# Stored low parts on the sync engine's DMA queue, their high parts from ScalarE

## The chip, the cores and the metric

The kernel runs on one core of a Trainium2 chip. The metric is the time of one execution in device microseconds; the median of several runs is compared. TensorE (PE) does the matmuls, VectorE (DVE) and ScalarE (ACT) the element-wise work, GpSimd (POOL) issues the DMAs that convert or accumulate, and SyncE (SP) issues the others.

## The reference

Two layers, each a mixer and an FFN, on x of 256 positions by 1024 features, in float32:

```python
for i in range(DEPTH):
    h = rms_norm(x, norm_mix[i])
    proj = einsum(h, w_in[i])      # qa ka va qb kb vb c_val c_gate qm, 256 columns each
    o_a = moba_attention(rope(norm(qa)), rope(norm(ka)), va)      # 4 heads of 64
    o_b = dilated_attention(rope(norm(qb)), rope(norm(kb)), vb)
    u = c_val * sigmoid(c_gate)
    o_c = silu(layer_norm(causal_depthwise_conv(u, conv_w[i]))) @ w_conv_out[i]   # 31 taps
    o_m = softmax(norm(qm) @ km.T) @ vm      # km, vm: from mem, with w_mem_kv[i]
    x = x + group_rms_norm([o_a, o_b, o_c, o_m]) @ w_out[i]
    h = rms_norm(x, norm_ffn[i])
    gate, val = split(causal_depthwise_conv(h @ w_up[i], ffn_conv_w[i]))   # 3 taps
    x = x + (silu(gate) * val) @ w_down[i]
```

## The kernel before, in words

**Three matmuls for one.** Every projection is made from a high and a low part of each operand, high·high + high·low + low·high (`mm3`). Weights come in units of 128 x 2048 float32, in two halves of 128 x 1024 (512 KB): `up0` to `up21` and `dn0` to `dn10` for the FFN, `qka`, `cg`, `qkb`, `cv`, `vv`, `qm` and `wo0` to `wo3` for a mixer (a pair such as `qka` is two units), and the small `co`. Three rings of SBUF slots hold halves: `st` (6 slots) as loaded, `wh` (7) the high parts, `wl` (7) the low parts.

**Three ways for a weight** (`get`, L725). The usual one: SP loads `st`, ACT copies it to `wh` in fp32r, DVE writes `wl` = `st` − `wh`; I call this last instruction the split of the half. The units in SOFT (L34): POOL loads `wh` with a converting DMA, ACT writes `wl` = −`wh`, and POOL's second DMA accumulates the weight onto it. The units in SPILL (L38) are for layer 1 alone: `wo1`, `wo0`, `qka` and `wo2`, ten halves. In FFN steps 3 to 12 of layer 0, one half a step, `spill` (L685) loads it, splits it, and stores the low part in a DRAM tile `sl` (`store`, L488, on POOL's queue). In layer 1 POOL loads the high part from the weights (`wh<-in_w`, converting) and the low part from the DRAM tile (`wl<-sl`).

**The stages.** The mixer of a layer (L1131) runs projections and attention in the order of ORDER (L44), the conv module's 31 taps on DVE beside them, and then the output projection `w_out` in three passes: groups b and a (PASSES' first entry, with `wo1` and `wo0`), memory (`wo3`), conv (`wo2`). The FFN (`ffn`, L1173) has 22 steps, each with an up projection, a gate, and the down projection of three steps earlier (LAG). Step 8 of layer 0 also makes the memory keys and values of layer 1 (`mem_kv`).

**What sets the order.** The whole program is first recorded as operations. A list scheduler (`schedule`, L492) then plans every engine's order from estimated durations, priorities (`key`) and free slots; it is rerun with priorities from the plan (`improve`, ITERS), and the best plan is emitted in that order. `get` and the spills put operations ahead by lowering `key`. SP's DMAs are chained in the order in which the program is recorded (`dma`, L475, through `dma_prev`), so SP's queue is never reordered; POOL's DMAs (`soft`, `store`) take any place that the plan gives them. A slot is free when its last use ends, in the plan 6.6 us later where that was a DMA of POOL (L568).

Instructions appear at L624 of `emit`, which issues all of them, but for the attention's matmuls (L622) and ACT's table loads (L618).

Of the kernel before, what the change touches and what calls it, by code (L numbers as in the profile page):

```python
# [10 lines left out]
F32 = mybir.dt.float32  # L11
F32R = mybir.dt.float32r
AF = mybir.ActivationFunctionType
ALU = mybir.AluOpType

P = 128
# [3 lines left out]
DEPTH = 2  # L20
# [9 lines left out]
HALF = UNIT // 2  # L30
# [5 lines left out]
RAW = ()  # L36

SPILL = ('wo1', 'wo0', 'qka', 'wo2')  # L38
SPILL_AT, SPILL_STEP = (3, 1)
LAG = 3  # L40

# [4 lines left out]
MEM_AT = 8  # L46
# [30 lines left out]
def unit_order():  # L77
    names = []
    for l in range(DEPTH):
        for s in ORDER[l]:  # L80
            names += [(l, s)] if s not in PAIRS or s == "mem" else []
            names += [(l, f"{s}{j}") for j in range(2)] if s in PAIRS else []
        for i, gs in enumerate(PASSES):
            if i == CO_AT:
                names += [(l, "co")]
            names += [(l, f"wo{g}") for g in gs]
        for i in range(NPAIR):
            names.append((l, f"up{i}"))
            if i == MEM_AT and l + 1 < DEPTH:
                names += [(l + 1, "mem"), (l + 1, "mem0"), (l + 1, "mem1")]  # L90
            if i >= LAG and (i - LAG) % 2 == 0:
                names.append((l, f"dn{(i - LAG) // 2}"))
        names += [(l, f"dn{j}") for j in range((NPAIR - LAG + 1) // 2, NPAIR // 2)]
    return names
# [224 lines left out]
LAT_CAST, LAT_ADD = 6600.0, 6600.0  # L319
# [4 lines left out]
class Rec:  # L324
# [160 lines left out]
        kw = dict(accum_op=ALU.add) if add else {}  # L485
        return self.op("pool", "dma_start", (out, src), kw, [out] if add else [], [out], 2200.0)

    def store(self, out, src):  # L488
        return self.op("pool", "dma_start", (out, src), {}, [src], [out], 2200.0)


    def schedule(self, slots):  # L492
        engs = ("pe", "act", "dve", "pool", "dma")
# [27 lines left out]
        while len(order) < len(self.ops):  # L521
            best = None
            for e in engs:
                cand = []
                for o in ready[e]:
                    t = possible(o)
                    if t is not None:
                        if o.table is not None and o.table != table[0]:
                            cand.append((t + TABLE_WAIT, o.key + TABLE_KEY, o.n, o, t))
                        else:  # L530
                            cand.append((t, o.key, o.n, o, t))
                if not cand:
                    continue
                t0 = min(c[0] for c in cand)
                c = min((c for c in cand if c[0] <= t0 + 1e-6), key=lambda c: (c[1], c[2]))
                if best is None or c[0] < best[0]:
                    best = c
            if best is None:
                raise RuntimeError("stuck: " + str([(e, [(o.meth, o.label, [(t.name, t.slot) for t in o.tiles])
                                                          for o in ready[e][:6]]) for e in engs]))  # L540
            o, t = best[3], best[4]
            ready[o.eng].remove(o)
            for l in o.tiles:
                if l.slot is None:
                    f = slot_free[l.tag]
                    f.sort(key=lambda x: x[:2])
                    l.slot, gate = f.pop(0)[1:]
                    o.gate.extend(gate)
                    turn[l.tag] = max(turn.get(l.tag, 0), l.seq + 1)
            dur = o.dur  # L550
            if o.table is not None and o.table != table[0]:
                dur += TABLE
                table[0] = o.table
            if o.eng == "pe":
                w = int(t // HAM)
                if w and busy.get(w - 1, 0.0) < COLD * HAM:
                    dur *= 2
                b = min(dur, (w + 1) * HAM - t)
                busy[w] = busy.get(w, 0.0) + b
                busy[w + 1] = busy.get(w + 1, 0.0) + dur - b  # L560
            o.start, o.end = t, t + dur
            free_at[o.eng] = o.end
            order.append(o)
            for l in o.tiles:
                l.left -= 1
                l.ops.append(o)
                if l.left == 0:
                    e = max(p.end + (LAT_CAST if p.eng == "pool" and p.meth == "dma_start" else 0.0) for p in l.ops)  # L568
                    slot_free[l.tag].append((e + LAT_X, l.slot, tuple(l.ops)))
            for q in o.nxt:  # L570
                q.wait -= 1
                q.ready = max(q.ready, o.end + q.prev[o])
                if q.wait == 0:
                    ready[q.eng].append(q)
# [76 lines left out]
class Kern:  # L651
# [33 lines left out]
    def spill(self, i):  # L685

        names = []
        for n in SPILL:
            names += [f"{n}{j}" for j in range(2)] if n in PAIRS else [n]
        if i >= 2 * len(names):  # L690
            return
        n, h = names[i // 2], i % 2
        r = self.r
        o = UOFF[(1, n)] * P
        src = self.d["w"][o:o + UNIT * P].rearrange("(p c) -> p c", p=P)[:, h * HALF:(h + 1) * HALF]
        st = self.t("st", [P, HALF], f"sp{n}{h}")
        r.dma(st, src, P * HALF * 4)
        hi, lo = self.t("wh", [P, HALF], f"sph{n}{h}", F32R), self.t("wl", [P, HALF], f"spl{n}{h}", F32R)
        self.split(hi, lo, st)
        d = self.t("sl", [P, HALF], f"sl{n}{h}")  # L700
        r.store(d, lo.bitcast(F32))
        self.spilled.setdefault(n, []).append((src, d))

    def unit(self, tag, cols, name, dtype=F32):
# [20 lines left out]
    def get(self, l, n, convert=True):  # L725
# [11 lines left out]
        soft = convert and spilled is None and (n in SOFT[l] or n[:-1] in SOFT[l]) and (l, n) not in self.staged  # L737
        if spilled is not None:
            hi, lo = self.unit("wh", cols, f"wh{l}{n}", F32R), self.unit("wl", cols, f"wl{l}{n}", F32R)
            self.r.key -= self.AHEAD  # L740
            for h, parts in enumerate(spilled):
                c = slice(h * HALF, (h + 1) * HALF)
                for out, src in zip((hi, lo), parts):
                    self.r.soft(out[:, c], src)
            self.r.key = save
            return hi, lo
        if not soft:
# [383 lines left out]
    def mixer(self, l, st, after):  # L1131
# [5 lines left out]
        for i, n in enumerate(ORDER[l]):  # L1137
# [24 lines left out]
            if 3 not in ys and "qm" in done and self.kv is not None:  # L1162
                base = r.key
                ys[3] = self.group_norm(self.attention(done["qm"], *self.kv, None, "m"), l, 3)
                self.kv = None
        for i, gs in enumerate(PASSES):
            if i == CO_AT:
                key, r.key = r.key, base
                ys[2] = self.group_norm(self.conv_out(l, y, self.get(l, "co")), l, 2)
                r.key = key  # L1170
            self.w_out(l, [(g, ys[g]) for g in gs], after if i == len(PASSES) - 1 else None)

    def ffn(self, l, st, after):  # L1173
# [14 lines left out]
        for i in range(NPAIR):  # L1188
# [2 lines left out]
                r.act(low[:, m, :], ps[:, 1, :], AF.Copy)  # L1191
                r.tt(us[:, m, :], ps[:, 0, :], low[:, m, :], ALU.add)
            if i == MEM_AT and l + 1 < DEPTH:
                self.kv = self.mem_kv(l + 1)
                self.gains(l + 1)
            if l == 0 and i >= SPILL_AT and (i - SPILL_AT) % SPILL_STEP == 0:
                self.spill((i - SPILL_AT) // SPILL_STEP)
            r.tt(us, us, st["rx"].twice(), ALU.mult)
            t = self.t2("tq")
            for c in range(2):  # L1200
# [19 lines left out]

    def build(self):
        r = self.r
        self.next_unit, self.staged, self.spilled = 0, {}, {}
        self.kv = None
        self.X = self.t("X", [P, NC, 256], "X")
        self.cst = self.t("cst", [P, NCST], "cst")
# [121 lines left out]
```

## Time and profile before

| | us |
|---|---|
| median of 3 runs (lowest to highest) | 623.24 (622.92 to 625.08) |
| the profiled execution | 623.19 |
| its span | 621.4 |
| PE busy | 608.0 (98% of the span) |
| DVE busy | 536.7 (86%) |
| ACT busy | 449.6 (72%) |
| POOL busy | 34.3 (6%) |

The span runs from the first to the last recorded instruction. PE was granted full clock throughout. Names such as `wh<-st` read "output from input", with the program's buffer names; in the orders below they carry the number of the buffer, so that one buffer can be followed.

### The profile page before, as it was taken

The page shows a single profiled execution, that of the slowest core. Times are in us where ns is not written, and L with a number is a line of the kernel's source. Part 1 is how long each engine was busy: PE and PEld are TensorE (multiplying, and loading weights), DVE is VectorE, ACT ScalarE, POOL GpSimd, SP SyncE. Part 2 cuts the span into 40 slices and gives each one's busy share as a digit, 9 for nine tenths or more (in the row PEclk, how much of TensorE's full clock was granted, in tenths as well). Part 3 has the DMA queues.
Part 4 walks back from the last instruction along what each step waited for, and adds up shares of the span by engine and source line. Part 5 has one row for each costly group of instructions (what it writes and reads, how often), then busy time and mean ns, then how long its engine had stood idle before and what let it go on. Part 6 is the DMA issues. An engine that isn't in the chain of part 4 may idle for free.

```text
span 621.4 us, 10750 instructions
## 1 busy us (share of the span) xinstructions
PE 608.0 (98%) x3884; PEld 537.0 (86%) x3884; DVE 536.7 (86%) x1048; ACT 449.6 (72%) x874; POOL 34.3 (6%) x63
## 2 busy tenths in 40 slices
PE   8999998999999999999999999899999999999997
PEld 5877876999998899999998878689899999999997
DVE  5899996899989999998869589849999888888874
ACT  6888969688776986766648488796776766666751
POOL 0001021000000000000020232100000000000000
PEclk9999999999999999999999999999999999999999
DMA  7987584676996899665685699606665565555401
GB/s 249 357 265 174 190 214 95 162 229 226 322 334 220 311 330 306 217 202 183 187 287 187 172 235 309 200 4 237 201 197 183 196 200 187 187 181 181 150 2 68
DMA packets 37493, 129.50 MB, mean 208 GB/s; under 512 B 4288, under 2 KB 5056, under 8 KB 37440
## 3 DMA queue, kind: packets, MB, share of 16 engines
q1 hardware_dynamic: 29664, 100.50, 48.7%
q0 software_dynamic: 7776, 28.32, 16.3%
q8 instruction: 30, 0.49, 0.3%
q14 instruction: 23, 0.19, 0.1%
HBM read 122.51 MB, written 6.29 MB: 207 GB/s over the span
## 4 chain that ended last, share of the span: by engine, by line
PE 80%; DVE 13%; ACT 3%; issue 2%; DMA 1%; SPq 1%; DVEq 0%; ACTq 0%
PE pj L624 55%; PE sc L624 10%; PE ss L624 8%; DVE y L624 5%; PE o L624 5%; DVE tq L624 1%; DVE wl L624 1%; DMA X<-in_x 1%; DVE tt L624 1%; PE o L622 1%; DVE pr L624 1%; ACT wh L624 1%; ACT pr L624 1%; DVE sm L624 1%; SPq L624 1%
## 5 line engine op out<-in xcount | busy, mean ns | idle before, releaser
L624 PE MATMUL pj<-HH,wh 128*128 128x512 f32 (+1 forms) x800 | 264.6, 380 | 0.0
L624 DVE TENSOR_TENSOR wl<-st,wh 128x1024 fp32r<-128x1024 f32 (+1 forms) x178 | 212.6, 1203 | 26.5 <-ACT wh L624 26.1
L624 ACT ACTIVATE wh<-st 128x1024 fp32r<-128x1024 f32 (+1 forms) x178 | 183.6, 1040 | 47.8 <-PE ss L624 31.2
L624 PE MATMUL pj<-HH,wl 128*128 128x256 f32 x752 | 210.8, 281 | 0.0
L624 PEld LDWEIGHTS pj<-HH,wh 128*128 128x128 f32 x800 | 147.0, 188 | 27.8
L624 PEld LDWEIGHTS pj<-HH,wl 128*128 128x128 f32 x752 | 142.1, 189 | 0.2
L624 PE MATMUL pj<-wh,HH 128*128 128x512 f32 (+1 forms) x320 | 95.4, 375 | 0.1
L624 DVE SCALAR_TENSOR_TENSOR tq<-tr,vec,tq 128x254 f32<-128x254 f32 (+1 forms) x176 | 75.0, 478 | 3.3 <-ACT tq L624 3.1
L624 PEld LDWEIGHTS pj<-wh,HH 128*128 128x128 f32 x320 | 58.2, 189 | 10.4 <-ACT v L624 0.5
L624 PE MATMUL pj<-wl,HH 128*128 128x512 f32 (+1 forms) x160 | 60.4, 379 | 0.5 <-DVE wl L624 0.5
L624 ACT ACTIVATE tq<-tr,vec 128x256 f32<-128x256 f32 x88 | 48.6, 591 | 14.0 <-DVE tr L624 13.9
L624 DVE SCALAR_TENSOR_TENSOR y<-upad,vec,y 128x256 f32<-128x256 f32 x120 | 51.6, 479 | 0.1
L624 PE MATMUL sc<-ah,wl 128*128 128x256 f32 x176 | 49.7, 283 | 0.0
L624 PE MATMUL sc<-al,wh 128*128 128x256 f32 x176 | 49.6, 283 | 0.0
L624 PE MATMUL sc<-ah,wh 128*128 128x256 f32 x176 | 49.0, 281 | 0.0
L624 ACT ACTIVATE tt<-pj 128x256 f32<-128x256 f32 x88 | 32.5, 371 | 21.4 <-PE pj L624 21.2
L624 DVE TENSOR_TENSOR tr<-pj,tt 128x256 f32<-128x256 f32 x88 | 36.7, 418 | 2.9 <-ACT tt L624 2.9
L624 ACT ACTIVATE pr<-pr,sm 128x256 f32<-128x256 f32 (+1 forms) x80 | 34.0, 459 | 3.5 <-DVE sm L624 3.4
L624 PEld LDWEIGHTS pj<-wl,HH 128*128 128x128 f32 x160 | 30.2, 189 | 7.3 <-issue 1.7
L624 PEld LDWEIGHTS sc<-ah,wh 128*128 128x128 f32 x176 | 33.1, 189 | 1.5
L624 PEld LDWEIGHTS sc<-ah,wl 128*128 128x128 f32 x176 | 33.1, 188 | 0.0
L624 PEld LDWEIGHTS sc<-al,wh 128*128 128x128 f32 x176 | 33.0, 188 | 0.0
(132 smaller groups left out, 991.4 us busy)
## 6 DMA issues: line engine op xcount, KB each, us to landing
st<-in_w SPq DMA_DIRECT2D x176, 512.0 KB, 4.6
wh<-in_w POOLq DMA_DIRECT2D x22, 512.0 KB, 7.1
wl<-in_w POOLq DMA_DIRECT2D x12, 512.0 KB, 7.7
sl<-wl POOLq DMA_DIRECT2D x10, 512.0 KB, 6.8
wl<-sl POOLq DMA_DIRECT2D x10, 512.0 KB, 8.0
st<-in_w SPq DMA_DIRECT2D x9, 256.0 KB, 7.0
st<-in_mem SPq DMA_DIRECT2D x4, 512.0 KB, 6.8
out_x<-X SPq DMA_DIRECT2D x4, 256.0 KB, 2.3
```

The lines of the kernel that those rows point to most:

```text
L622: nc.tensor.matmul(real(out), real(lhsT), real(rhs), start=start, stop=stop, skip_group_check=True)
L624: getattr(engs[o.eng], o.meth)(*[real(a) for a in o.args], **{k: real(v) for k, v in o.kw.items()})
```

## The change

The method `store` goes, and `spill` no longer stores: it notes the pair of DRAM tile and low part. At the next FFN step, ahead of that step's own spill, `ffn` issues the noted store with `r.dma`, that is in SP's chain. In layer 1, where `get` had two DMAs of POOL for each half, SP loads the half into `st`, ACT copies it to `wh`, and SP loads the low part from the DRAM tile. (The branch `cast` keeps the converting DMA for units that are in layer 1's SOFT; none of the four is.) The operations no longer lower `key` by AHEAD. A slot last used by a DMA of SP counts as free 2.0 us later in the plan (LAT_DMA). The rest is inert: MEM1 is None and SPILL_PER is 1.

```diff
@@ schedule
-    e = max(p.end + (LAT_CAST if p.eng == "pool" and p.meth == "dma_start" else 0.0) for p in l.ops)
+    e = max(p.end + (0.0 if p.meth != "dma_start" else LAT_CAST if p.eng == "pool" else LAT_DMA) for p in l.ops)
@@ spill
-        r.store(d, lo.bitcast(F32))
+        self.stores.append((d, lo))
         self.spilled.setdefault(n, []).append((src, d))
@@ get
         if spilled is not None:
             hi, lo = ...
-            self.r.key -= self.AHEAD
-            for h, parts in enumerate(spilled):
+            cast = n in SOFT[1] or n[:-1] in SOFT[1]
+            if cast:
+                self.r.key -= self.AHEAD
+            for h, (src, d) in enumerate(spilled):
                 c = slice(h * HALF, (h + 1) * HALF)
-                for out, src in zip((hi, lo), parts):
-                    self.r.soft(out[:, c], src)
+                if cast:
+                    self.r.soft(hi[:, c], src)
+                else:
+                    st = self.t("st", [P, HALF], f"st{l}{n}{h}")
+                    self.r.dma(st, src, P * HALF * 4)
+                    self.r.act(hi[:, c], st, AF.Copy)
+                self.r.dma(lo[:, c].bitcast(F32), d, P * HALF * 4)
@@ ffn, once a step, ahead of self.spill(...)
+            late, self.stores = self.stores, []
+            for d, x in late:
+                r.dma(d, x.bitcast(F32), P * HALF * 4)
```

What the plan makes of it is seen in the emitted orders. Over the program POOL's DMAs go from 54 to 24, SP's grow by 30, ACT has ten more `wh<-st` copies of a half and 16 table loads in place of 14; the instructions of PE and DVE are the same in kind and number.

SP in layer 0's FFN, from the first step with a store on; `st` are loads, `sl` stores, and in brackets stand the queues and engines that each waits for. Before:

```order
L624 DMA st_70<-in_w 128x1024 [waits DMAHW2_49,DVE_49]
L624 DMA st_72<-in_w 128x1024 [waits DMAHW3_49,DVE_49]
L624 DMA st_68<-in_w 128x1024 [waits DMAHW4_49,DVE_49]
L624 DMA st_71<-in_w 128x1024 [waits DMAHW5_49,DVE_49,Activation_49]
L624 DMA st_69<-in_w 128x1024 [waits DMAHW6_49,DVE_49]
L624 DMA st_67<-in_w 128x1024 [waits DMAHW7_49,DVE_49,Activation_49]
```

The same place after:

```order
L625 DMA st_69<-in_w 128x1024 [waits DMAHW0_49,DVE_49,Activation_49]
L625 DMA sl_147<-wl_86 128x1024 [waits DVE_49]
L625 DMA st_67<-in_w 128x1024 [waits DMAHW1_49,Activation_49]
L625 DMA st_70<-in_w 128x1024 [waits DMAHW2_49,Activation_49]
L625 DMA st_72<-in_w 128x1024 [waits DMAHW3_49,DVE_49]
L625 DMA sl_148<-wl_84 128x1024 [waits DVE_49]
L625 DMA st_68<-in_w 128x1024 [waits DMAHW4_49,Activation_49]
L625 DMA st_71<-in_w 128x1024 [waits DMAHW5_49,Activation_49]
L625 DMA st_69<-in_w 128x1024 [waits DMAHW6_49,Activation_49]
L625 DMA st_67<-in_w 128x1024 [waits DMAHW7_49,DMAHW0_49,Activation_49]
L625 DMA st_70<-in_w 128x1024 [waits DMAHW1_49,DVE_49]
L625 DMA sl_149<-wl_80 128x1024 [waits DVE_49]
```

Three stores now stand between the loads, with three and five loads between them, and each waits for DVE.

ACT in layer 1's mixer, at the softmax of group b (`pr`, `sm`, `pt`), the values `v` and the weights. Before:

```order
L624 ACTIVATE pr_122,sm_126<-pr_122,sm_126 128x256
L624 ACTIVATE pr_122,sm_126<-pr_122,sm_126 128x128
L624 ACTIVATE v_118<-pj_157,rt_96 128x512
L624 ACTIVATE pr_122<-pr_122,sm_126 128x128
L624 ACTIVATE pr_122<-pr_122,sm_126 128x256
L624 ACTIVATE v_118<-pj_158,rt_96 128x512
L624 ACTIVATE pr_120,sm_127<-pr_120,sm_127 128x256
L624 ACTIVATE pr_120,sm_127<-pr_120,sm_127 128x128
L624 ACTIVATE pt_123<-ss_160 128x384
L624 ACTIVATE pt_124<-ss_161 128x384
L624 ACTIVATE pr_120<-pr_120,sm_127 128x128
L624 ACTIVATE pr_120<-pr_120,sm_127 128x256
```

After:

```order
L625 ACTIVATE wh_74<-st_67 128x1024
L625 ACTIVATE pr_122,sm_126<-pr_122,sm_126 128x256
L625 ACTIVATE pr_122,sm_126<-pr_122,sm_126 128x128
L625 ACTIVATE wh_79<-st_70 128x1024
L625 ACTIVATE v_118<-pj_159,rt_96 128x512
L625 ACTIVATE v_118<-pj_157,rt_96 128x512
L625 ACTIVATE pr_122<-pr_122,sm_126 128x128
L625 ACTIVATE pr_122<-pr_122,sm_126 128x256
L625 ACTIVATE pr_120,sm_127<-pr_120,sm_127 128x256
L625 ACTIVATE pr_120,sm_127<-pr_120,sm_127 128x128
L625 ACTIVATE pt_123<-ss_160 128x384
L625 ACTIVATE pt_124<-ss_161 128x384
```

Two copies `wh<-st` of a half stand here that were not there (`wh_74`, `wh_79`); a third, `wh_75`, follows three instructions on.

DVE in layer 1's mixer, just ahead of the output projection: `y` are conv taps, `tt` and `al` the scaled outputs of groups a and b and their low parts, `s` and `sm` with TENSOR_REDUCE the sums and maxima of the memory attention. Before:

```order
L624 TENSOR_TENSOR al_139<-tt_111,ah_133 128x256
L624 SCALAR_TENSOR_TENSOR y_129<-upad_66,vec_65,y_129 128x256
L624 TENSOR_TENSOR tq_105<-pj_159,gm_103 128x512
L624 SCALAR_TENSOR_TENSOR y_129<-upad_66,vec_65,y_129 128x256
L624 TENSOR_REDUCE s_101<-ts_107 128x8
L624 TENSOR_TENSOR t_113<-ts_106 128x256
L624 SCALAR_TENSOR_TENSOR y_129<-upad_66,vec_65,y_129 128x256 x2
L624 TENSOR_TENSOR al_140<-tt_111,ah_134 128x256
L624 SCALAR_TENSOR_TENSOR y_129<-upad_66,vec_65,y_129 128x256 x2
L624 SCALAR_TENSOR_TENSOR tt_110<-o_164,vec_65,t_112 128x256 x2
L624 TENSOR_REDUCE sm_125<-sc_162 128x2
L624 TENSOR_TENSOR al_138<-tt_110,ah_131 128x256
```

After, where `t_113` and one tap stand right ahead of the first row:

```order
L625 TENSOR_REDUCE sm_125<-sc_162 128x2
L625 SCALAR_TENSOR_TENSOR y_129<-upad_66,vec_65,y_129 128x256
L625 TENSOR_TENSOR sm_125<-sm_125,s_101 128x2
L625 TENSOR_REDUCE sm_126<-sc_163 128x2
L625 SCALAR_TENSOR_TENSOR tt_110<-o_164,vec_65,t_112 128x256
L625 SCALAR_TENSOR_TENSOR y_129<-upad_66,vec_65,y_129 128x256
L625 SCALAR_TENSOR_TENSOR tt_110<-o_164,vec_65,t_112 128x256
L625 TENSOR_TENSOR al_139<-tt_110,ah_131 128x256
L625 RECIPROCAL sm_125<-sm_125 128x2
L625 TENSOR_TENSOR sm_126<-sm_126,s_101 128x2
L625 TENSOR_TENSOR al_140<-tt_111,ah_133 128x256
L625 TENSOR_TENSOR al_138<-tt_110,ah_132 128x256
```

The low parts `al` made of `tt_111`, two of which stood ahead of the last two `tt_110`, come behind them now, and both reduces of `sc` stand ahead of them.

## Rows read from the trace of the kernel before

**Rows 1.** Busy time of each engine over the span, its share, and instructions.

```profile
PE 608.0 (98%) x3884; PEld 537.0 (86%) x3884; DVE 536.7 (86%) x1048; ACT 449.6 (72%) x874; POOL 34.3 (6%) x63
```

**Rows 2.** Busy time by stretch: stretch, length, then each engine's; after PEclk the DMA share.

```profile
core 0: us, PE busy (x) PEld busy (x) DVE busy (x) ACT busy (x) POOL busy (x), PEclk, DMA share, GB/s
361.50:373.00 11.50, 10.93 (x60) 7.63 (x59) 11.32 (x43) 10.64 (x32) 4.27 (x6) 1.00 1.02 213
373.00:388.00 15.00, 14.89 (x103) 11.93 (x102) 15.00 (x50) 12.19 (x35) 4.62 (x8) 1.00 1.07 308
388.00:397.20 9.20, 7.52 (x48) 4.71 (x47) 9.20 (x24) 5.64 (x14) 1.59 (x3) 1.00 0.93 296
300.00:326.00 26.00, 26.00 (x188) 24.58 (x187) 18.45 (x37) 13.78 (x29) 4.25 (x8) 1.00 0.79 254
115.00:260.00 145.00, 144.99 (x919) 131.65 (x918) 141.72 (x244) 112.65 (x200) 5.37 (x10) 1.00 0.81 273
185.00:215.00 30.00, 29.99 (x179) 26.40 (x178) 29.96 (x58) 24.40 (x47) 1.06 (x2) 1.00 0.78 261
```

**Rows 3.** The stores on POOL: ns of one (min/median/max), first and last start.

```profile
L624 POOL DMA_DIRECT2D sl<-wl x10: 531/531/562, 136.9 to 232.6; - x10
```

**Rows 4.** Waits, whole program: engine and line, for whom; us, times, longest.

```profile
POOL sl L624 <- DVE wl L624: 121.8, 10, 31.0
...
DVE wl L624 <- ACT wh L624: 26.1, 46, 0.7
...
ACT wh L624 <- DMA st<-in_w: 5.2, 6, 1.8
```

**Rows 5.** Loads of st on SP: ns of one issue, first and last start.

```profile
L624 SPq DMA_DIRECT2D st<-in_w x187: 327/328/1073, 1.6 to 582.7; - x187
```

**Rows 6.** The longest group of waits of SP's queue, 115 to 260 us.

```profile
SPq L624 <- DVE wl L624: 103.4, 43, 14.6
```

**Rows 7.** Work on tile wl alone, 115 to 260 us; DVE's 62 are the splits.

```profile
115.00:260.00 145.00, 106.89 (x375) 70.66 (x375) 73.22 (x62) 0.00 (x0) 5.37 (x10) 1.00 0.81 273
```

**Rows 8.** DMA issues: how many, size of one, median us from issue to landing.

```profile
st<-in_w SPq DMA_DIRECT2D x176, 512.0 KB, 4.6
...
sl<-wl POOLq DMA_DIRECT2D x10, 512.0 KB, 6.8
wl<-sl POOLq DMA_DIRECT2D x10, 512.0 KB, 8.0
st<-in_w SPq DMA_DIRECT2D x9, 256.0 KB, 7.0
```

**Rows 9.** Timeline of ACT near 327.6: two copies of a half, one after the other.

```profile
327.63 2.00 ACT L624 ACTIVATE wh<-st 128x1024 fp32r<-128x1024 f32 x2
```

**Rows 10.** Timeline of ACT near 338: one table load.

```profile
337.92 1.28 ACT L618 ACT_TABLE_LOAD   x1
```

**Rows 11.** Timeline of POOL: the last low half of qka is issued.

```profile
317.78 0.53 POOL L624 DMA_DIRECT2D wl<-sl  x1 [0.29 <-DVE tq L624]
```

**Rows 12.** Timeline of PE: the first matmul of layer 1's qka.

```profile
325.26 0.39 PE L624 MATMUL pj<-wh,HH 128*128 128x512 f32 x1
```

**Rows 13.** Timeline of DVE ahead of the output projection; x2 is two in a row.

```profile
394.28 0.88 DVE L624 SCALAR_TENSOR_TENSOR y<-upad,vec,y 128x256 f32<-128x256 f32 x2
395.07 0.87 DVE L624 SCALAR_TENSOR_TENSOR tt<-o,vec,t 128x256 f32<-128x256 f32 x2
395.86 0.68 DVE L624 TENSOR_REDUCE sm<-sc 128x2 f32<-128x512 f32 x1
396.46 0.75 DVE L624 TENSOR_TENSOR al<-tt,ah 128x256 fp32r<-128x256 f32 x2
397.13 0.48 DVE L624 SCALAR_TENSOR_TENSOR y<-upad,vec,y 128x256 f32<-128x256 f32 x1
```

**Rows 14.** Timeline of PE at the start of the output projection.

```profile
397.39 0.28 PE L624 MATMUL pj<-al,wh 128*128 128x256 f32 x1
397.51 0.28 PE L624 MATMUL pj<-ah,wl 128*128 128x256 f32 x1
```

More of the change, by code (lines that the diff above doesn't have):

```diff
@@ L38 @@
 SPILL = ('wo1', 'wo0', 'qka', 'wo2')
+MEM1 = None
+SPILL_PER = 1
 SPILL_AT, SPILL_STEP = (3, 1)
@@ L83, in unit_order @@
         for i, gs in enumerate(PASSES):
+            if i == MEM1 and l + 1 < DEPTH:
+                names += [(l + 1, "mem"), (l + 1, "mem0"), (l + 1, "mem1")]
             if i == CO_AT:
@@ L88, in unit_order @@
             names.append((l, f"up{i}"))
-            if i == MEM_AT and l + 1 < DEPTH:
+            if MEM1 is None and i == MEM_AT and l + 1 < DEPTH:
                 names += [(l + 1, "mem"), (l + 1, "mem0"), (l + 1, "mem1")]
@@ L486, in soft @@
         return self.op("pool", "dma_start", (out, src), kw, [out] if add else [], [out], 2200.0)
-    def store(self, out, src):
-        return self.op("pool", "dma_start", (out, src), {}, [src], [out], 2200.0)
     def schedule(self, slots):
@@ L1166, in mixer @@
         for i, gs in enumerate(PASSES):
+            if i == MEM1 and l + 1 < DEPTH:
+                key = r.key
+                r.off = OFFS.get((l + 1, "mem"), 0.0)
+                self.kv = self.mem_kv(l + 1)
+                r.off = 0.0
+                r.key = key
             if i == CO_AT:
@@ L1193, in ffn @@
             if i == MEM_AT and l + 1 < DEPTH:
-                self.kv = self.mem_kv(l + 1)
+                if MEM1 is None:
+                    self.kv = self.mem_kv(l + 1)
                 self.gains(l + 1)
+            late, self.stores = self.stores, []
+            for d, x in late:
+                r.dma(d, x.bitcast(F32), P * HALF * 4)
             if l == 0 and i >= SPILL_AT and (i - SPILL_AT) % SPILL_STEP == 0:
-                self.spill((i - SPILL_AT) // SPILL_STEP)
+                for q in range(SPILL_PER):
+                    self.spill((i - SPILL_AT) // SPILL_STEP * SPILL_PER + q)
             r.tt(us, us, st["rx"].twice(), ALU.mult)
@@ L1222, in build @@
         r = self.r
-        self.next_unit, self.staged, self.spilled = 0, {}, {}
+        self.next_unit, self.staged, self.spilled, self.stores = 0, {}, {}, []
         self.kv = None
```

## The prediction

> **What bounds the kernel now.** I read the busy times first, then them again by stretch, then the waits, the DMA issues, and last the timeline where a term hangs on it. TensorE (PE) is busy 608.0 of 621.4 us [rows 1], so its own work is nearly the whole time, and only stretches in which PE idles, or could be made to idle, can move. The stretches [rows 2] show three kinds. In 115 to 260 us, the FFN steps of layer 0 that hold all ten spills, PE is busy 144.99 of 145 us: PE sets the pace. But VectorE (DVE) is busy 141.72 there, so it has 3.28 us to spare in ten steps, and 0.04 us in 185 to 215 us. In 300 to 326 us (end of that FFN, norm of layer 1) PE is full again, while DVE (18.45 of 26) and ScalarE (ACT, 13.78 of 26) have room. In 361.5 to 397.2 us (attention and conv of layer 1, ahead of its output projection) it is the other way round: DVE is busy 11.32 + 15.00 + 9.20 = 35.52 of 35.70 us, PE 10.93 + 14.89 + 7.52 = 33.34. There DVE sets the end: it works through conv taps, softmax and splits without a gap, while ACT has 0.86 + 2.81 + 3.56 = 7.23 us free.
>
> So the change can act in two places: it can starve DVE in the spill stretch, where 3.28 us of lateness is all that is absorbed, or move ACT's and DVE's work in the stretch that ends at 397.2.
>
> **The change part by part.** The sum starts from the profiled execution: span 621.4, the whole 623.19, so 1.8 us lie around the span; the median is 623.24.
>
> 1. POOL loses thirty DMAs (ten each of wh<-in_w, sl<-wl, wl<-sl). A store takes 0.53 us of POOL [rows 3], and POOL is busy 34.3 us in all [rows 1]. It stood 121.8 us waiting for the ten splits that it was to store [rows 4], and nobody waited for it. Removing this gives 0.
>
> 2. The sync queue (SP) gains thirty DMAs at 0.327 us of issue [rows 5], 9.8 us over two stretches; in the spill stretch it waits 103.4 us for DVE's splits anyway [rows 6]. Its load costs 0; its order is the question.
>
> 3. The stores stand in SP's order now. In the first order piece, each waits for the split of a half that was loaded a few places earlier, and all later loads stand behind it. Before, a load needs only its st slot, so SP runs six halves ahead. Splits follow each other every 145 / 62 = 2.34 us [rows 7], so six halves are 14.0 us of cover. Now three and five loads stand between stores, in turn. The load right behind a store cannot be issued before the stored half is split; where three stand between, its own split is due about three halves later: 3 × 2.34 = 7.0 us of cover. It needs 0.33 us of issue, 4.6 us to land [rows 8], and 1.0 us of ACT for the high part (two copies in 2.00, [rows 9]): 5.9 us. The cover holds by 1.1 us, and I take 0. The far end comes from slower landings in the same view. With 7.0 us (the 256 KB loads) the need is 8.3, 1.3 late; five tight stores make 6.5, less the 3.28 us that DVE can absorb: +3.2. With 8.0 us (loads of the stored tiles by POOL) it is 9.3, 2.3 late: 5 × 2.3 − 3.28 = +8.2. I take 0 because 512 KB loads of this very queue land in 4.6. A gain is excluded: PE has 0.01 us to give.
>
> The order also has two more table loads on ACT around the memory keys of step 8 (16 against 14 in the program), 1.28 us each [rows 10]; ACT is busy 24.40 of 30 us in 185 to 215, so I take 0, with 2.6 as the far end.
>
> What [rows 4] shows of a store is its wait: up to 31.0 us at the head of POOL's queue. The Trainium skill (DMA: Bandwidth & Descriptors, section "Issuing engines are not separate DMA queues") says that transfers of all issuing engines run on the same 16 DMA engines, and that another issuer only saves its issue time, usually small. By that rule alone this part costs 0 with no far end; it speaks of transfers, and says nothing of what stands behind a waiting instruction.
>
> 4. The first stored weights that are used again are qka. Before, the last of their four low halves is issued at 317.78 [rows 11], and PE takes the weights up from 325.26 [rows 12]. On SP the issue is bound by the same freed slot, so it lands at 317.78 + 0.33 + 4.6 = 322.7, or with 8.0 us at 326.1. I take 0, at most +0.8.
>
> 5. Ten more high parts on ACT, 1.0 us each. Four (qka) fall in 300 to 326, where ACT has 12.2 us free: 0. Six belong to the output projection. Four of these stand among the softmax work of group b (three of them in the second order piece): 4.0 us against 2.81 us of idle ACT in 373 to 388, so 1.2 us of softmax, and of what hangs on it on DVE, comes later. The ends: 0, if the 3.56 us after 388 take it, and 6.0, if nothing covers the six. I take +1.2, from the idle time of that very stretch.
>
> 6. DVE's instructions are the same in number and shape; just ahead of the output projection they stand otherwise (third order piece). By starts [rows 13], a tap takes 0.40 us, a `tt` 0.40, a reduce 0.60, an `al` 0.33. From `t` to the end of the first `al` made of tt_110, which PE needs first, it was four taps, one al, two tt, a reduce and that al: 1.6 + 0.33 + 0.8 + 0.6 + 0.33 = 3.66. Now it is three taps, two reduces, two tt, a small one (0.1) and that al: 1.2 + 1.2 + 0.8 + 0.1 + 0.33 = 3.63; and one al that stood ahead of `t` comes behind. So PE can begin 0.33 + 0.03 = 0.36 us earlier. But the second al of tt_110 now comes 0.86 us after the first (two small ones, two al) against 0.33, and the fourth has two additions on y ahead of it, 0.8 more; PE, which takes a matmul every 0.12 us [rows 14] and has six or seven between, stands for some 0.1 to 0.2 at each. Together about 0, ends −0.4 and +0.5.
>
> Sum: 623.2 + 1.2 = **624.4 us**.
>
> **The rivals.** (a) *Slower: the store's wait takes SP's read-ahead away.* If the load behind a store lands after ACT and DVE need it, DVE idles, and beyond 3.28 us of lost time PE idles with it. For it speaks that DMA is busy at 0.81 of its engines in that stretch, at 273 GB/s [rows 2], with the stores in that already, and that other loads took 7.0 and 8.0 us [rows 8]. Against it stands the 1.1 us that part 3 leaves. Price: +3.2 to +8.2 on the sum, 627.6 to 632.6, with 630 in the middle.
>
> (b) *Faster: the new order feeds PE better between 361.5 and 397.2.* PE stands 35.70 − 33.34 = 2.36 us there, and POOL is rid of twelve loads that stood among the other weights it fetches. If ACT's copies cost nothing and PE's idle time came back with the 0.4 us of part 6, that is 623.2 − 2.8 = 620.4; if matmuls that are now spread out also close up, below 620.1. Against it: DVE has 0.18 us free in that stretch and no instruction fewer.
>
> A related mechanism: a store takes POOL 531 ns in the median and 562 at most [rows 3], beside a DVE at 141.72 of 145 us. The Trainium skill (SBUF — State Buffer, section "SBUF: two separate sides") has GpSimd and some DVE operations shut each other out of a port that they share. If that cost DVE anything here, taking the DMAs from POOL would be a gain of (b)'s kind. With stores that vary by 31 ns the trace does not show it.
>
> (c) *Nothing moves:* the copies are covered, 623.2. It differs from the forecast by less than can be told apart.
>
> That the change does not do what it says is excluded by the order: ten stores and ten loads stand on SP, ten more copies on ACT, and POOL keeps 24 of 54 DMAs.
>
> **How the numbers follow.** A measurement of this kernel tells apart about 0.5%, 3.1 us: faster means below 620.1, slower above 626.4. The forecast together with (c), 620.1 to 626.4: 0.60. Rival (a), with the ends of parts 3 and 5: 0.28, because the cover is only 1.1 us of 7.0 and hangs on one landing time. Rival (b) in full: 0.12. So faster 0.12, same 0.60, slower 0.28. The range leaves out about 0.1 on each side, most of (b) and the upper half of (a): 620.1 to 630.0.
>
> **What would show it.** In the profile of the changed kernel: PE full in 115 to 260 as before, DVE's wait for ACT's high parts no longer than 0.7 us at a time and ACT's for its st loads 1.8 [rows 4], though SP's own waits differ; the first use of layer 1's qka still near 325.3; six wh<-st copies between 373 and 397; the output projection's matmuls with al about 1 us later than those of [rows 14]. The forecast is wrong if ACT waits for st loads by several us in the steps with a store, and DVE and PE behind it (then (a)), or if the stretch up to 397.2 ends sooner with DVE's work in it the same (then (b)).

## The result

The changed kernel takes 634.97 us in the median (4 runs, 631.76 to 638.54), before 623.52: 1.0169 times as long, interval 1.0138 to 1.0200. Run again in another comparison (e18_again below) it took 634.95 us, 1.0184 times (1.0153 to 1.0214). The forecast was 624.4 with a range to 630.0: slower by 11.45 us where "no change" was the likeliest case.

Its profiled execution took 638.54 us, the longest of its four; its span is 636.4, 15.0 more than before. The page's busy times (compare [rows 1]), then stretches (columns as in [rows 2]):

```profile
PE 614.5 (97%) x3884; PEld 541.7 (85%) x3884; DVE 537.9 (85%) x1048; ACT 459.8 (72%) x886; POOL 18.3 (3%) x33
```

```profile
core 0: us, PE busy (x) PEld busy (x) DVE busy (x) ACT busy (x) POOL busy (x), PEclk, DMA share, GB/s
115.00:260.00 145.00, 141.97 (x882) 127.93 (x881) 136.63 (x232) 111.28 (x195) 0.00 (x0) 0.99 0.77 262
215.00:220.00 5.00, 3.68 (x15) 3.22 (x16) 4.29 (x11) 3.94 (x11) 0.00 (x0) 0.66 0.66 248
361.50:397.20 35.70, 31.41 (x206) 24.76 (x205) 28.32 (x93) 28.05 (x71) 5.90 (x8) 1.00 1.02 298
405.00:410.00 5.00, 3.08 (x14) 1.82 (x12) 3.85 (x10) 3.02 (x10) 0.00 (x0) 0.81 0.16 62
410.00:415.00 5.00, 5.00 (x26) 4.65 (x28) 3.25 (x11) 4.26 (x14) 0.00 (x0) 0.66 0.11 25
```

PE has the same 3884 matmuls, but its busy time grew by 6.5 us and its idle time by 8.5. In the FFN of layer 0 (115 to 260) PE lost 3 us where it had lost nothing. From 361.5 to 397.2 DVE, which had been without a gap, is busy only 28.32 us; in 367.9 to 403.7, 6.4 us further on, it is 30.48 of 35.80. It no longer sets the pace there. And in three short stretches the granted clock is 0.66 to 0.81.

Where the time went is read from one instruction that both have: the last `tr<-tr,rx` of layer 0's FFN, on DVE's timeline before and after (start, duration):

```profile
314.82 0.69 DVE L624 TENSOR_TENSOR tr<-tr,rx 128x512 f32<-128x512 f32 x1
```

```profile
321.25 0.69 DVE L625 TENSOR_TENSOR tr<-tr,rx 128x512 f32<-128x512 f32 x1
```

By then it is 6.4 us late; the other 8.6 come behind it, all before the first steps of layer 1's FFN are through, after which the distance stays. I call these **the loss in layer 0** and **in layer 1**; the table below has them for every run. They are from one profiled execution each, and executions of one kernel differ by some us (e18_again: 4.1 and 7.8).

Part of the loss in layer 0 lies ahead of its FFN, and of every store. One of the last additions onto x in layer 0's mixer comes 1.4 us late in the change, and the granted clock over 95 to 100 us is 0.66 there against 1.00 before. The addition, then the stretch, each before and after:

```profile
114.64 0.68 DVE L624 TENSOR_TENSOR X<-X,pj 128x512 f32<-128x512 f32 x1
```

```profile
116.08 0.68 DVE L625 TENSOR_TENSOR X<-X,pj 128x512 f32<-128x512 f32 x1
```

```profile
95.00:100.00 5.00, 3.86 (x24) 2.32 (x24) 4.85 (x15) 4.78 (x15) 0.00 (x0) 1.00 0.12 24
```

```profile
95.00:100.00 5.00, 4.60 (x19) 2.92 (x20) 4.85 (x15) 3.73 (x11) 0.00 (x0) 0.66 0.21 41
```

In e18_again, the same kernel, that clock is 1.00 and the same addition stands at 113.79, 0.9 us earlier than before. So this part belongs to the execution and not to the change. The table's figures still hold it. Without it the FFN of layer 0 loses 5.0 and 4.9 us in the two executions of the change, 4.8 in e7 and 3.7 in e9.

PE's gaps, on its timeline (in brackets the gap ahead of the instruction, and what ended it):

```profile
216.32 0.69 PE L625 MATMUL ss<-cst,tq 128*128 128x128 f32 x2 [2.81 <-DVE tq L625]
```

```profile
380.83 0.50 PE L625 MATMUL pj<-wl,HH 128*128 128x512 f32 x1 [1.37 <-DMA wl<-in_w]
...
387.01 0.50 PE L625 MATMUL pj<-wl,HH 128*128 128x512 f32 x1 [2.03 <-DMA wl<-in_w]
...
390.79 0.39 PE L625 MATMUL pj<-wl,HH 128*128 128x256 f32 x1 [0.33 <-DMA wl<-in_w]
...
402.92 0.63 PE L625 MATMUL ss<-cst,tq 128*128 128x128 f32 x4 [1.71 <-DVE tq L625]
...
410.00 0.98 PE L625 MATMUL ss<-y,fill 128*128 128x256 f32 x2 [1.92 <-DVE y L625]
```

The first is at step 8 of layer 0's FFN. The next three are the projections vv and qm, which wait for low parts that POOL loads; the last two are ahead of the output projection. Waits (columns as in [rows 4]) and DMA issues (as in [rows 8]):

```profile
DVE wl L625 <- ACT wh L625: 30.0, 51, 1.3
...
ACT wh L625 <- DMA st<-in_w: 15.1, 15, 2.1
...
PE pj L625 <- DMA wl<-in_w: 3.7, 3, 2.0
```

```profile
st<-in_w SPq DMA_DIRECT2D x186, 512.0 KB, 4.9
...
sl<-wl SPq DMA_DIRECT2D x10, 512.0 KB, 3.2
```

ACT's wait for loads went from 5.2 us in 6 times to 15.1 in 15, and DVE's longest wait for a high part from 0.7 us to 1.3: the marks that I had named for rival (a).

### The profile page after: what moved, and what is told of

Same layout as the page of the kernel before. It is cut to its first block, busy times and chain, and to the rows that moved or that the text cites. A ratio compares the mean times of both kernels' runs of the same rounds, so it can differ in the third digit from the quotient of the medians.

```text
span 636.4 us, 10736 instructions
## 1 busy us (share of the span) xinstructions
PE 614.5 (97%) x3884; PEld 541.7 (85%) x3884; DVE 537.9 (85%) x1048; ACT 459.8 (72%) x886; POOL 18.3 (3%) x33
## 4 chain that ended last, share of the span: by engine, by line
PE 66%; DMA 11%; DVE 10%; ACT 8%; issue 4%; SPq 1%; POOL 1%; DVEq 0%; POOLq 0%; ACTq 0%
PE pj L625 45%; PE sc L625 8%; PE ss L625 7%; DMA st<-in_w 7%; PE o L625 4%; ACT wh L625 3%; DVE wl L625 2%; DMA wh<-in_w 2%; DVE y L625 2%; DVE tq L625 2%; ACT pr L625 1%; DMA st<-in_mem 1%; PE sc L623 1%; PE o L623 1%; DMA cst<-in_cst 1%
## 5 line engine op out<-in xcount | busy, mean ns | idle before, releaser
L625 DVE TENSOR_TENSOR wl<-st,wh 128x1024 fp32r<-128x1024 f32 (+1 forms) x178 | 212.4, 1201 | 30.1 <-ACT wh L625 30.0
L625 ACT ACTIVATE wh<-st 128x1024 fp32r<-128x1024 f32 (+1 forms) x188 | 194.2, 1041 | 55.9 <-PE ss L625 31.0
```

Of the source, the lines that this page charges most:

```text
L625: getattr(engs[o.eng], o.meth)(*[real(a) for a in o.args], **{k: real(v) for k, v in o.kw.items()})
```

## The experiments

Each median stands beside that of the kernel before in the same comparison. "Old priorities" means that the planner was given the final priorities of the kernel before; "old plan", that PE, DVE and ACT have exactly its order.

| run | what it is | us (before) | ratio, interval | loss in layer 0 / 1, us |
|---|---|---|---|---|
| the change | | 634.97 (623.52) | 1.0138 to 1.0200 | 6.4 / 8.6 |
| e18_again | the change again | 634.95 (623.81) | 1.0153 to 1.0214 | 4.1 / 7.8 |
| e1_stores_pool | its plan, stores on POOL | 639.10 (624.55) | 1.0215 to 1.0266 | 10.9 / 7.1 |
| e17_right_place | its plan, stores later on SP | 641.73 (623.81) | 1.0243 to 1.0310 | 13.3 / 4.9 |
| e2_only_stores | stores alone, replanned | 629.04 (624.55) | 1.0055 to 1.0089 | 6.8 / 0.7 |
| e3_only_get | loads alone, replanned | 635.77 (624.55) | 1.0142 to 1.0212 | 6.0 / 7.7 |
| e6_replan_cast | nothing but replanned | 628.76 (623.78) | 1.0055 to 1.0127 | 5.4 / 0.5 |
| e8_replan_dma | nothing but replanned | 627.24 (623.78) | 1.0035 to 1.0075 | 3.7 / 0.5 |
| e5_sp_old_plan | stores on SP, old plan | 623.76 (623.78) | 0.9980 to 1.0020 | 1.5 / −0.2 |
| e13_chain3 | the same, three loads behind each | 655.23 (624.48) | 1.0478 to 1.0529 | 31.2 / −0.2 |
| e9_stores_one_step | stores alone, old priorities | 627.82 (623.41) | 1.0043 to 1.0089 | 4.3 / 0.9 |
| e10_stores_two_steps | stores a step later still | 627.67 (623.41) | 1.0041 to 1.0079 | 7.2 / −0.2 |
| e7_old_priorities | all, old priorities | 636.14 (623.78) | 1.0151 to 1.0220 | 4.8 / 7.7 |
| e4_small_wo | transfers of wo cut | 631.87 (624.55) | 1.0083 to 1.0150 | 4.1 / 1.0 |
| e11_late_wo_loads | all, loads of wo later | 634.73 (623.41) | 1.0160 to 1.0232 | 4.5 / 6.8 |
| e12_both_late | both cures | 634.87 (623.41) | 1.0164 to 1.0206 | 4.4 / 8.2 |
| e16_get_both | loads alone, old priorities | 630.49 (624.48) | 1.0084 to 1.0141 | −0.1 / 5.4 |
| e14_lo_only | low parts alone on SP | 627.45 (624.48) | 1.0033 to 1.0071 | −0.8 / 3.7 |
| e15_hi_only | high parts alone over ACT | 625.66 (624.48) | 1.0001 to 1.0034 | 0.8 / 0.3 |

### First round: the parts apart

The theory was that of rival (a) in two places, stores that wait on SP and loads that get in each other's way; its rival, that the order made anew costs the time.

**e1_stores_pool.** The plan stays; at emission the store goes to another queue:

```diff
-            getattr(engs[o.eng], o.meth)(...)
+            getattr(engs[o.via or o.eng], o.meth)(...)     # via = "pool" for the ten stores
```

> The changed kernel with its own plan, word for word, but the ten stores are issued from POOL's queue instead of SP's. Queue theory: the FFN of layer 0 lost 6.4 us (its last step's gate input comes at 321.95 instead of 315.51) because loads stand behind stores that wait for a split; with the stores off SP that lateness is under 1.5 us, the 2.81 us gap of PE at step 8 and the lower clock behind it are gone, and the time is 626 to 630. Rival, plan theory: the new order itself (two more table loads, other places of splits) costs it whatever queue issues the stores: the time stays at 632 to 638 and the gap at step 8 stays.

It got slower, beyond both expectations, and a gap at step 8 stays (1.81 us, behind others of 2.66 and 1.06). ACT's waits for loads are back at the level of before, but a new wait stands in their place:

```profile
ACT wh L626 <- DMA st<-in_w: 5.6, 6, 2.0
...
DVE wl L626 <- DMA sl<-wl: 4.0, 2, 3.8
```

The plan of the change frees the slot of a stored low part 2.0 us after the store; from POOL a store lands in 6.8 us [rows 8], here too, and DVE waits for the slot. So the run says nothing on the queue; it says that this plan depends on quick stores.

**e2_only_stores, e3_only_get.** One half of the change each. In e2 `get` is that of before; e3 against the changed kernel:

```diff
-        self.stores.append((d, lo))
+        r.op("pool", "dma_start", (d, lo.bitcast(F32)), {}, [lo.bitcast(F32)], [d], 2200.0)
```

> The kernel before with the stores alone changed (SP, one step late), the loads of layer 1 as before on POOL; the plan is made anew. Queue theory: about the loss of layer 0's FFN, 4 to 7 us: 627 to 631, with the mixer of layer 1 as before. Plan theory, or all of it from layer 1: 623 to 624.

> The changed kernel with the stores as before (POOL, at once), the loads and ACT copies of layer 1 as changed; the plan is made anew. If the loss in layer 1 (8.5 us between 322 and 462 us of the changed kernel) is its own: 629 to 633, with layer 0 as before. If it only follows from the late FFN of layer 0: 623 to 625.

Each half alone costs, 4.5 and 11.2 us, the second more than either expectation had. The loss in layer 1 belongs to the loads alone (7.7 against 0.7). But layer 0 loses 6 us in both, also in e3, whose layer 0 has the stores and queues of before. That spoke for the order.

**e4_small_wo.**

```diff
+                if n[:2] == "wo":
+                    o1.via = o2.via = 64     # columns moved, of 1024
```

> The changed kernel with its own plan; of the twelve transfers of the stored output projection weights in layer 1 (six high, six low halves) only 64 of 1024 columns are moved, so those weights are mostly not loaded; queues, waits and ACT's copies stay. Transfer theory: POOL's weights for vv and qm, which PE waits for at 379, 385 and 390 us (3.7 us), land 3 us earlier or more, the two later gaps (1.71 and 1.92 us) and the lower clock behind them go, and the time falls by 6 to 10 us, to 625 to 629. Copy theory (my part 5: the six copies take ACT's time in the softmax): nothing falls but by 1 us, 632 to 638.

Only 64 of 1024 columns move in each of these transfers, so the run leaves most of the output projection's stored weights out. In the profiled execution (628.63 us, the shortest of four) the loss in layer 1 falls to 1.0 us, with no gap at pj<-wl,HH. The median is 7.3 us above the kernel beside it, where that of the change is 11.45 above its own: 4.1 us less, which is less than either the profile or the theory has it. So by the medians about half of the loss in layer 1 hangs on the bytes of these loads, not on the time of ACT's copies, which all stay. How they cost shows in the time from issue to landing of POOL's accumulating loads, in the stretch in which vv and qm are loaded, 355 to 390 us before and 360 to 395 after (columns as in [rows 8]):

```profile
wl<-in_w POOLq DMA_DIRECT2D x5, 512.0 KB, 7.7
```

```profile
wl<-in_w POOLq DMA_DIRECT2D x6, 512.0 KB, 10.5
```

7.7 us became 10.5, since SP's loads of the output projection are on the same DMA engines at the same time; in e4, without most of their bytes, it is 7.4 (360 to 395). Before, they stood behind vv and qm in POOL's own queue. The rule of the Trainium skill (DMA: Bandwidth & Descriptors, section "Issuing engines are not separate DMA queues") that all issuers share the 16 DMA engines agrees with this.

### Second round: the order

**e5_sp_old_plan.** The kernel before with `via = "dma"` for its stores, so that SP issues each where the old plan had POOL's.

> The kernel before with its own plan, word for word; only the ten stores are issued by SP, where the plan has POOL's store. Queue theory: SP stands for the splits, the loads behind each store come late, and the FFN of layer 0 loses 3 to 7 us: 627 to 631. Plan theory (the loss in layer 0 is the new order, not the queue): within 1.5 us of before, 623 to 626, no gap of PE over 1 us between 200 and 220 us.

1.000: issued in these places, the ten stores cost nothing on SP's queue, and my part 2 holds for the stores. It has 1.5 us of loss in its profile, 0.9 of it before the first store, where its clock over 95 to 100 us is 0.66 as well.

**e6_replan_cast, e8_replan_dma.** One constant of the planner:

```diff
-LAT_CAST, LAT_ADD = 6600.0, 6600.0
+LAT_CAST, LAT_ADD = 6400.0, 6600.0      # e6; in e8 LAT_DMA 2000.0 -> 2050.0
```

> The kernel before with nothing changed but a constant of the planner (6.4 instead of 6.6 us for the latency of POOL's DMAs), so that the plan is made anew; stores and loads are all as before. It has 16 table loads, as the changed kernel has. Plan theory: a gap of PE of 2 to 3 us at step 8 of layer 0's FFN and 4 to 7 us by its end, 627 to 631. Queue theory: 623 to 625.

> As the run with 6.4 us, but another constant: 2.05 instead of 2.0 us for the latency of SP's DMAs in the plan. Plan theory: 626 to 631, with the gap at step 8 (16 table loads again). Queue theory: 623 to 625.

Planning anew, with nothing changed on any queue, costs 5.0 and 3.5 us. PE's gap at step 8 is there in both, here in e6, with ACT's table loads of that stretch:

```profile
214.71 0.69 PE L624 MATMUL ss<-cst,tq 128*128 128x128 f32 x2 [3.11 <-DVE tq L624]
```

```profile
199.35 1.28 ACT L618 ACT_TABLE_LOAD   x1
...
207.07 1.28 ACT L624 ACT_TABLE_LOAD   x1
...
213.16 1.28 ACT L618 ACT_TABLE_LOAD   x1
...
215.50 1.28 ACT L624 ACT_TABLE_LOAD   x1
```

The old order has one pair of table loads there; the new ones put a switch back and forth, and copies, ahead of the small ACT work on the memory keys. In the change it is the same: table loads at 206.35 and 213.70, then the 2.81 us gap. That the table loads make the gap is not shown: on the chain of work that ended last they stand in the change and, with the one at 212.30, in e8, but in e6 that chain runs over DVE's splits instead. That stretch had no DVE time to spare [rows 2].

**e7_old_priorities.** The operations of before are recorded and planned first, and their priorities given on:

```diff
-        best = self.improve(slots)
+        best = b.improve(slots)      # b: the operations of the kernel before
+        for o in r.ops:
+            o.key = marked[o.mark] if o.mark else keys[o.eng].pop(0)
```

> The changed kernel, all its operations and queues, but planned with the final priorities of the kernel before (a new operation has that of the one that it replaces), so that the order is as near to that of before as the change allows (14 table loads). Plan theory: layer 0 within 2 us of before, the loss of layer 1 (7.6 us, from the transfers) as it was: 629 to 633. Queue theory: both losses stay, 634 to 638.

With 14 table loads, as before, layer 0 still loses 4.8 us and PE still stands 2.57 us at step 8. So the order made anew isn't all of it, and neither are the two added table loads: the plan theory missed, too. All of the change, planned so, costs 12.4 us; the loss does not need the new order.

### Third round: cures

e9 to e12 keep the old priorities; e9 has the stores of the change and the `get` of before. The edits of e10 and of e11, both of which e12 has:

```diff
-            late, self.stores = self.stores, []
+            late, self.stores, self.fresh = self.stores, self.fresh, []     # e10; spill appends to fresh
...
+                    if n == "wo1" and h == 0:                               # e11; gate: qm's last high part
+                        self.r.act(st[:, :1], self.gate, AF.Copy)
                     self.r.dma(st, src, P * HALF * 4)
```

> Planned with the priorities of the kernel before: the stores alone as changed (SP's chain, one step late), the loads of layer 1 as before on POOL. Chain theory (a store that stands too early in SP's chain holds up the loads behind it, though SP's queue itself costs nothing): the FFN of layer 0 ends 4 to 6 us late, as it did with all of the change and these priorities (+4.8), layer 1 adds nothing: 627 to 630. Plan theory: 623 to 625.

> The same, but each store is put two FFN steps late in SP's chain, so that its split is done when SP comes to it. Chain theory: ACT's waits for loads fall back to under 6 us and the FFN of layer 0 ends within 2 us of before: 623 to 626. Rival (the low part that is held a step longer takes a wl slot from the ring, and DVE waits for slots): 626 to 630.

> All of the change with the priorities of before (636.1 us in its run), and one element copied by ACT onto the first st tile of wo1 after ACT's work on the last half of qm, so that SP starts the loads of the output projection only then, behind POOL's weights for vv and qm. No byte and no DMA less. Order theory (the loads cost because they share the DMA engines with weights that PE needs first): PE's gaps at pj<-wl,HH (4.1 us) are under 1 us and the loss in layer 1 falls from 7.4 to under 3.5 us: 629 to 633. Copy theory (ACT's copies and its waits for st): 635 to 638.

> Both cures at once: all of the change with the priorities of before, the stores two steps late, the loads of the output projection behind those of qm. If the two theories hold the whole loss: 623 to 627. If something else remains, above 628.

e9: the stores alone cost 4.4 us, with ACT waiting 16.3 us for loads. e10 is no cure, as its rival said: the waits for loads fall, but the low part that is held longer now keeps others waiting (3.4 us of its 7.2 are there before the first store, at a clock of 0.67 and 0.65 in 95 to 105 us):

```profile
ACT wh L626 <- DVE wl L626: 12.6, 6, 3.8
...
ACT wh L626 <- DMA st<-in_w: 6.9, 9, 1.9
...
DVE wl L626 <- DMA sl<-wl: 5.3, 3, 2.1
```

e11 takes PE's waits for vv and qm away, as order theory said, but the loss stays at 6.8 us. It only moves: the high parts now come late for ACT's copies, which stand in ACT's queue ahead of the softmax of group b. First ACT, then PE:

```profile
391.21 1.06 ACT L626 ACTIVATE wh<-st 128x1024 fp32r<-128x1024 f32 x1 [3.12 <-DMA st<-in_w]
```

```profile
393.38 0.55 PE L626 MATMUL ss<-cst,pr 128*128 128x128 f32 x3 [2.93 <-ACT pt L626]
```

ACT stands 3.12 us for a load, and behind that copy PE stands 2.93 for `pt`. e12 adds nothing to this: both cures together leave 11.5 us.

### Fourth round: what was still open

**e13_chain3.** e5, and in the finished order, for each store s:

```diff
+            for o in moved:              # the three loads of SP next ahead of s
+                r.order.remove(o)
+            k = r.order.index(s) + 1
+            r.order[k:k] = moved
```

> The kernel before with its own plan, word for word for PE, DVE and ACT; the stores are issued by SP, and the three loads that stood ahead of each store in SP's order stand behind it, so that each store comes about as early in SP's chain as in the changed kernel. Chain theory (a store that is reached before its split holds up the loads behind it): ACT's waits for loads grow from 5 to over 10 us, the FFN of layer 0 ends 2 to 5 us late, 626 to 629. Plan theory (only the new order costs): 623 to 625.

The same ten stores on the same queue cost 0 in one place and 31 us three loads earlier. That is far more than the 2 to 5 us expected, so the run shows that the place costs, not what it costs in the change. The wait that shows it, and one of PE's gaps:

```profile
ACT wh L625 <- DMA st<-in_w: 44.1, 20, 5.3
```

```profile
232.82 0.50 PE L625 MATMUL pj<-HH,wh 128*128 128x512 f32 x1 [4.06 <-ACT vm L625]
```

**e14_lo_only, e15_hi_only, e16_get_both.** The old priorities and the stores of before; e16 has the `get` of the change, e14 and e15 half of it:

```diff
-                    self.r.dma(st, src, P * HALF * 4)          # e14
-                    self.r.act(hi[:, c], st, AF.Copy)
+                    self.r.soft(hi[:, c], src)
...
-                self.r.dma(lo[:, c].bitcast(F32), d, P * HALF * 4)     # e15
+                self.r.soft(lo[:, c], d)
```

> Planned with the priorities of before, stores as before; in layer 1 the low parts are loaded by SP, the high parts by POOL's converting DMAs as before. Low-part theory (SP's loads share the DMA engines with POOL's weights): 627 to 631. High-part theory (the cost is the way over st and ACT's queue): 623 to 625.

> As the run before it, but the other half: the high parts go over SP, st and an ACT copy, the low parts are loaded by POOL as before. High-part theory: 627 to 632, with ACT waiting for st loads in the softmax or PE for vv and qm. Low-part theory: 623 to 625.

> Planned with the priorities of before, stores as before, both high and low parts in layer 1 as changed. If the loss in layer 1 does not need the late FFN: layer 0 within 1 us of before, layer 1 loses 6 to 8 us, 629 to 632. If it comes only with a late FFN: 623 to 626.

Layer 0 is within 1 us of before in all three. The loads cost 6.0 us alone: the low parts on SP 3.0, the high parts over ACT 1.2, the two together more than the sum.

**e17_right_place, e18_again.** The change with its own plan, each store up to three loads later on SP (not past a use of its slot):

```diff
+            r.order.insert(last + 1, s)     # last: the third load of SP behind s
+            r.order.pop(k)
```

> The changed kernel with its own plan, word for word for PE, DVE and ACT; each store stands up to three loads later in SP's order, about where the exact old plan had it for nothing. If the stores' waits are the loss of layer 0 in the changed kernel: ACT's waits for loads fall from 15 to about 5 us and the FFN of layer 0 ends at most 2 us late instead of 6, the time falls by 4 us or more against the kernel beside it. If the order made anew is: the gap at step 8 and 4 to 6 us stay, the time within 1.5 us of the kernel beside it.

> The changed kernel itself, beside the other on the same chip: 632 to 638, with the FFN of layer 0 ending 5 to 7 us late and a gap of PE at step 8.

```profile
DVE wl L626 <- DMA sl<-wl: 12.9, 5, 6.1
...
ACT wh L626 <- DMA st<-in_w: 4.8, 7, 1.1
```

As in e1, the waits for loads go (4.8 us) and waits for the stored part's slot come (12.9 us): 6.8 us slower than the change beside it, which neither expectation had. In the plan of the change a store is too early for the loads and, put later, too late for the slots.

## Why the prediction was wrong

**What the runs settle.** The loads alone cost 6.0 us with layer 0 as before (e16). The stores alone cost 4.4 with nearly the old order (e9). Together that is 10.4 of the 11.45 us, and both at once, planned with the same priorities, cost 12.4 (e7). In layer 0 the trace of the change shows how. In the kernel before, the chain of work that ended last is PE alone from 115 to 225 us. In the change it leaves PE at 150.42 and is back at 216.32, behind the gap; on the way stand three loads that were issued behind stores, and both table loads (start, us; the last table load and PE's return below them):

```profile
151.60 5.65 DMA st<-in_w
...
160.04 6.60 DMA st<-in_w
...
169.97 6.62 DMA st<-in_w
...
213.70 1.28 ACT L619
...
216.32 0.69 PE ss L625 x2
```

ACT stood 1.9, 2.1 and 0.6 us for these loads; the first two on its timeline:

```profile
157.28 1.06 ACT L625 ACTIVATE wh<-st 128x1024 fp32r<-128x1024 f32 x1 [1.92 <-DMA st<-in_w]
...
166.72 1.06 ACT L625 ACTIVATE wh<-st 128x1024 fp32r<-128x1024 f32 x1 [2.12 <-DMA st<-in_w]
```

The chain of e18_again has the same pieces (loads of 5.72, 6.09 and 6.82 us, table loads at 203.81 and 211.16). In e6 and e8, with no store on SP, it has one load in this stretch. So both the wait on SP and ACT's order lie on the path to the gap in the change itself.

**What stays open:** how the loss in layer 0 of the changed kernel divides between the two. Either alone gives 3.5 to 5 us in the same steps (e9; e6, e8), and together they did not give the sum; e1 and e17, which were to part them, brought in a wait of their own.

Parts 1 and 2 hold as far as they were tried. No run shows a gain from POOL's thirty DMAs, and a split takes 1201 ns on average against 1203. What the Trainium skill (SBUF — State Buffer, section "SBUF: two separate sides") says, that GpSimd and some DVE operations shut each other out of a port that they share, is not seen here. SP's issue time cost nothing for the ten stores (e5); the other twenty DMAs were not tried apart from their transfers.

Part 3 is the first step that failed: the term was 0, with rival (a) beside it. The mechanism was named rightly. Its margin of 1.1 us was the mistake, on both sides. For the landing I took 4.6 us, the median of the whole program, though the same view gives more for the stretch that the stores are in (115 to 260 us, before, then after):

```profile
st<-in_w SPq DMA_DIRECT2D x64, 512.0 KB, 5.9
```

```profile
st<-in_w SPq DMA_DIRECT2D x61, 512.0 KB, 6.4
```

With 5.9 us, which the trace before already had, the need is 7.2 us against a cover of 7.0; with the 6.6 us that two of the loads on the chain took it is 7.9. And the cover, taken from the mean distance of the splits, was shorter in its place: ACT was ready for the first two of these loads 3.8 and 4.6 us after their issue, where 7.0 less the copy's 1.0 is 6.0. The 3.28 us that DVE had to spare did not take the delay up: 0.04 of them lay in 185 to 215, through which the chain runs without a load, over DVE and ACT, to the gap. The far end, +3.2 at a landing in 7.0 us, is near to e9's 4.4, in part by luck: it was priced at five late stores, and up to 225 us the chain of the change has three late loads, that of e9 one. The 634.97 us lie above all of rival (a), 627.6 to 632.6, as that has no wait for loads in layer 1.

The two table loads, taken at 0 because ACT had time in that stretch, were not hidden in the change: both are on that chain, ahead of work that PE waits for, and ACT's idle time elsewhere does not pay for that. They are not the whole gap: e7 and e9, with 14 table loads, stand 2.57 and 1.73 us at the same place. More widely, I treated the new order as the old one with small edits. The order of before was worth 3.5 and 5.0 us against two that were planned anew, and an edit to what is planned can give that up.

Part 4 looked at qka only, where the loss is small (a gap of 0.69 us at 326.10; 1.9 in e18_again). It missed that the same move puts the output projection's loads beside POOL's weights for vv and qm: 3.7 us of PE's waits at once. And the output projection's own loads land late. One of them is on the chain that ended last, and through the copy of it in ACT's queue PE's gap ahead of 402.92 hangs on it:

```profile
386.01 14.18 DMA st<-in_w
...
400.21 1.06 ACT wh L625
```

In e18_again the chain goes the same way, over a load of 14.67 us. This was no rival of mine, and it is the larger half.

Part 5 was right: 1.2 us forecast, 1.2 in e15 (interval 0.1 to 2.1), where PE stands 1.21 us for the softmax's `pt`, behind two of the copies. That the figures agree so closely is partly luck, since e15 also puts loads of SP beside POOL's. Part 6 cannot be told from the rest, since late loads set the end there now.

## What to carry to other kernels

Of an instruction that waits in an in-order queue, find its place in the queue's time, not in the program's: the same ten stores cost nothing or 31 us. Where one queue issued all transfers of a stage, their order was an asset; a second queue for some of them lets them take DMA time from what is needed first. Take a landing time from the stretch where it counts, not from the whole program. And where a planner makes the order, time a kernel that is planned anew with nothing changed, before any difference is put down to the edit.

## What was not expected of the hardware

A gap of PE can cost more than its length, and need not. Behind the 2.81 us gap the granted clock is 0.66 over 215 to 220 us; by single microseconds it is at 0.50, the lower level of 1.2 GHz, up to 219, and at 1.00, 2.4 GHz, from 220:

```profile
218.00:219.00 1.00, 1.00 (x5) 0.90 (x4) 1.00 (x3) 0.67 (x2) 0.00 (x0) 0.50 0.20 74
...
220.00:221.00 1.00, 1.00 (x8) 0.86 (x7) 0.55 (x1) 1.00 (x2) 0.00 (x0) 1.00 0.99 340
```

Eight matmuls of one projection take 2.44 us there, the next eight 1.41, by the chain of waits (start, duration):

```profile
217.01 2.44 PE pj L625 x8
...
219.66 1.41 PE pj L625 x8
```

In e18_again the same gap is 2.81 us long, too, but the clock stays at 1.00 behind it, and these eight take 1.57. In 405 to 415, behind gaps of 1.71 and 1.92 us, it is 0.81 and 0.66; in e18_again, behind gaps of 1.45 and 2.10 us, 0.74 and 0.92. My prices for the rivals counted the gaps alone.

A store of 512 KB lands in 3.2 us in the change, where SP issues it, and took 6.8 from POOL [rows 8]. The queue alone does not decide it: the stores of e5 and e10, on SP too, take 4.1 and 7.0.
